# Two gate groups of a hybrid attention layer computed with the activations stationary, and the first loads split over two queues

## The chip, the cores and the metric

The kernel runs on one core of a Trainium2 chip. It is written in a language in which each engine has its own in-order list of instructions: TensorE (PE, matrix products; its weight loads are shown apart as PEld), VectorE (DVE), ScalarE (ACT), GpSimd (POOL) and SyncE (SP). SyncE, GpSimd and ScalarE also issue DMA transfers, each from its own queue. The metric is the device time of one execution in microseconds (us); less is better. Columns streamed by a product are the elements per partition of its moving operand.

## The reference

Two layers work on 256 tokens of width 2048. One input projection of a layer gives eleven parts: queries, keys, values and a gate for eight heads of chunked attention (A); queries, keys, values, a gate and a low-rank forget gate for four heads of gated linear attention (B, "GLA" below); queries and a gate for four heads that attend to 256 memory tokens (M). Each part's output is multiplied by its SiLU gate, and one output projection maps the three back to width 2048.

```python
h = x @ w_in
a_q, a_k, a_v, a_z, b_q, b_k, b_v, b_z, b_lr, m_q, m_z = jnp.split(h, cuts, axis=-1)
y_a = chunk_band_attention(heads_a(a_q), heads_a(a_k), heads_a(a_v), rel_table)   # 8 heads of 128
log_g = log_sigmoid(b_lr @ gate_w + gate_b) / 16
y_b = rms_norm(gla_chunk_recurrence(b_q, b_k, b_v, log_g)) * gla_norm_g           # 4 heads
mk, mv = jnp.split(mem @ w_mem_kv, 2, axis=-1)
y_m = memory_attention(heads_m(m_q), mk, mv)                                      # 4 heads of 128
y = jnp.concatenate([y_a * silu(a_z), y_b * silu(b_z), y_m * silu(m_z)], axis=-1)
x = layer_norm(DEEPNORM_ALPHA * x + y @ w_out, ln_g, ln_b)
```

The sizes are float32 throughout. The part that matters below is `y_a * silu(a_z)`: 1024 columns, which the kernel computes as two groups of 512, `G_AZ0` and `G_AZ1`.

## The kernel before, in words

**Products in three.** Every operand of a large product is split into a high and a low part (`parts`: ScalarE casts the high part, line 117; VectorE subtracts it, line 118), and a product is high times high, low times high and high times low. All such products are issued by the helper `mm`, line 95, so in the profile nearly every product of TensorE bears L95; the tile tells what it belongs to. `acc` is the accumulator of a large group of 512 output columns, `bk` one bank for a head's work or other small work, `wh` and `wl` the two parts of a weight piece, `x` an operand of activations (`xq` the input, `memq` the memory, `yq` the gated output; four tiles each), held transposed, with the contraction on partitions.

**Two forms of a group.** `as_group` keeps the activations stationary: for each of 16 contraction tiles and each half of the 256 tokens, three products of 512 columns (96 in all, in eight pieces of 12); the result has tokens on partitions. `ws_group` keeps the weights stationary: for each contraction tile and each block of 128 output columns one product of 512 columns (the weights' high part on both parts of `x`) and one of 256 (their low part on the high part of `x`), 64 and 64 in eight pieces of 16; its result has output columns on partitions, which is the form in which the heads give their output. Before, `G_AK0`, `G_AK1` and the three gates `G_AZ0`, `G_AZ1` and `G_MZ` are weights-stationary groups. `ws_group` yields two halves; for each, `total` (lines 262 and 263) adds its two sums.

**Turned.** Where a result is needed the other way round, `turned` does it without TensorE: VectorE transposes in blocks of 32 (line 521), GpSimd's queue stores the block to DRAM (`home`, line 523) and reads it back in four loads (line 526) that complete the transposition. Probabilities of a head (`pT`), the GLA output (`yT`) and the queries (`yr`, `qk`) go this way.

**What sets the order.** TensorE's order is that in which the program issues its work. The large groups come one after another: memory keys and values, `G_BQK` (GLA queries and keys), values, queries and keys of A, `G_MQ`, then the gate stage `G_BZ`, `G_AZ0`, `G_AZ1`, `G_MZ`, then the four groups of the output projection `G_WO`. After each piece a group calls `tick`, which advances the generators of the heads: each yields the number of pieces after which it wants its next step. `tick` steps at most one generator per piece, at most two or three are active, and the others stand in `waiting`. A head's step is a visit on TensorE between two pieces: its scores, and about 7 to 9 pieces later the product of its probabilities with the values. `finish(gens)` calls `tick` until the named generators are done. VectorE's and ScalarE's orders are set by a scheduler with priorities; weight pieces (`piece`: loads on SyncE's queue, line 142, and their split) have a high one. There are four buffers of raw pieces and four of each part, so the loads are always some pieces ahead of TensorE. GpSimd's queue is in order too, and its order comes from the scheduler.

**The gate stage before.** `G_BZ` is activation-stationary; its gate multiplies the GLA output with tokens on partitions (`gla_gate`), and `gla_turned` then turns that in two halves and splits it into `yq[0]`. For the three other gates the loop shown in the diff takes both halves' sums through SiLU, calls `finish` for the heads whose output they gate, multiplies (line 901) and splits into `yq[1]` to `yq[3]`. In layer 0 the four loads of the norm's two rows for all partitions (`gb`, lines 917 and 918, on GpSimd's queue) stand in the program in each group of the output projection; their first use is in layer 1, in `restored` (line 632).

**The start.** `zeros` feeds six products whose result nobody reads; they stand ahead of the first real product. `first_pieces` loads, for the first contraction tiles, a block of the memory (`res<-memT`, line 165, into the space that the residual takes later), its value weights (line 178, the very first block in two halves of 256 columns) and its key weights (line 180), in this order and all on SyncE's queue. `gla_inputs` loads the forget gate's weights three times into a 48-row tile (`gwraw`, line 305), its bias (`gb`, line 309) and the GLA norm (`ng`, line 310) on GpSimd's queue. `G_BQK` is followed there by `ident` and `lm`, two constants on SyncE's queue (lines 828 and 830).

Of the kernel before, what the change touches and what calls it, by code (L numbers as in the profile page):

```python
# [36 lines left out]
def hybrid_trunk_kernel(  # L37
# [12 lines left out]
    waiting, active, done, now, linear = [], [], set(), [0], []  # L50
# [103 lines left out]
    def first_pieces(p, x):  # L154
# [9 lines left out]
        def x_part(j):  # L164
            sp.dma_start(xraw[:, j], xsrc[:, j])  # L165
            parts(x[0][:, j], x[1][:, j], xraw[:, j])
# [4 lines left out]
        if p < 2:  # L171
            with tc.manual_schedule(engines={DVE, mybir.EngineType.Activation}):
                for k in range(2):
                    x_part(slice(j0 + k, j0 + k + 1))
                    cut = 2 if p == k == 0 else 1
                    for h in range(cut):
                        cs = slice(h * 512 // cut, (h + 1) * 512 // cut)
                        sp.dma_start(raws[0][:, k, cs], vsrc[:, k, cs])  # L178
                        split(0, (slice(None), k, cs))
# [12 lines left out]
    def first_memory(mk, mv, each):  # L192
# [6 lines left out]
        def values_of(p, w, kk):  # L199

            for h in range(2 if p == kk == 0 else 1):
                cs = slice(h * 256, h * 256 + 256) if p == kk == 0 else slice(0, 512)
                for t in range(2):
                    as_products(accv[:, t, cs], t, memq, [x[:, :, cs] for x in w], p * 2 + kk, kk, -1 if h else 0)
# [93 lines left out]
    def gla_inputs(l):  # L298
# [5 lines left out]
        for i in range(3):  # L304
            pool.dma_start(raw[i * 16:i * 16 + 16], gate_w[l])  # L305
# [3 lines left out]
        pool.dma_start(gb, gate_b[l])  # L309
        pool.dma_start(ng, norm_g[l])  # L310
# [181 lines left out]
    def gla_turned(yraw, ng, y):  # L492

        yT = []
        for par in range(2):
            yT.append(hd.tile([P, 4, P], F32, name=nm("yT"), tag=("gq", "gk")[par]))
            turned(P, (yT[par], yraw[:, 2 * par:2 * par + 2].rearrange("p t d -> p (t d)")))
            yield 6
        for par in range(2):
# [6 lines left out]
            yield 1  # L506

# [270 lines left out]
    for _ in range(6):  # L778
# [6 lines left out]
    for l in range(L):  # L785
# [3 lines left out]
        def staged(g, x, raw, place):  # L789
# [4 lines left out]
            active.append((gen, now[0] + 5))  # L794
# [95 lines left out]
        waiting[:0] = gens[0]  # L890
        for i, g in ((1, G_AZ0), (2, G_AZ1), (3, G_MZ)):
            y = operand()
            gates = []
            for j, a, b in ws_group(w512[l, g], xq):
                sz = scratch([P, 2, T])
                total(sz, a, b)
                act.activation(sz, sz, AF.Silu)
                gates.append((j, sz))
            finish(gens[i])
            for j, sz in gates:  # L900
                dve.tensor_tensor(sz, sz, yraw[i][:, j:j + 2], op=ALU.mult)
                parts(y[0][:, j:j + 2], y[1][:, j:j + 2], sz)
            yq.append(y)
# [5 lines left out]
        gb = []  # L909
        rows = norm_rows(l) if last else None  # L910
        for n in range(WO_N):
            if last:
                g, b = scratch([P, 512]), scratch([P, 512])
            else:
                both = per.tile([P, 2, 512], F32, name=nm("gb"), tag=f"yr{n}")
                g, b = both[:, 0], both[:, 1]
            pool.dma_start(g, ln_g[l:l + 1, columns(n)].to_broadcast([P, 512]))
            pool.dma_start(b, ln_b[l:l + 1, columns(n)].to_broadcast([P, 512]))
            gb.append((g, b))
# [28 lines left out]
            acc = as_group(src, yq, 512)  # L948
# [5 lines left out]
        if not last:  # L954
            norm_between(stats)
# [87 lines left out]
```

## Time and profile before

| what | value |
|---|---|
| time, median of 3 runs | 910.96 us (910.96 to 911.66) |
| the profiled execution's own time | 911.12 us |
| its span in the profile | 909.3 us |
| granted TensorE clock over the span | 0.998 |
| TensorE busy | 902.5 us (99%) |
| weight loads busy (beside products) | 783.0 us (86%) |
| VectorE, ScalarE, GpSimd busy | 606.7, 486.0, 148.1 us |
| DMA traffic | 200.86 MB, mean 221 GB/s |
| packets' share of 16 engines: hardware queue q1, software queue q0 | 60.5%, 10.2% |
| gate stage, layer 0 / layer 1 (end of `G_BZ` to end of `G_MZ`) | 292.0 to 364.0 / 739.8 to 811.7 us |

A busy time is the sum over an engine's instructions of one execution. The chain of waits is followed back from the last instruction, at each step to what released it; a row of it gives start, duration, engine, tile, line and number of instructions. A row of the timeline gives the same for one engine and, in square brackets, how long it had been idle and what it waited for. A row of the windows gives the stretch, its length, the busy time of PE, PEld, DVE, ACT and POOL with their instructions, the granted clock, the DMA engines' busy share and GB/s. A row of the waits says which engine waited for what: total us, number, longest.

### The profile page before, as it was taken

Reading aid. Unit: us, or ns where it says so; the run is one execution under the profiler, and the core shown is the slowest. Engines: PE = TensorE matmul, PEld = TensorE weight load, DVE = VectorE, ACT = ScalarE, POOL = GpSimd, SP = SyncE. Lnnn points to the kernel's source line nnn. Section 1 sums busy time; section 2 is a strip of 40 time slices with the busy share of each in tenths; the row PEclk is TensorE's granted clock in tenths of the full one; section 3 lists DMA queues with packets and bytes.
Section 4 is the critical chain, followed back from the end, with each engine's and each line's share of the span. In section 5 each row is a group of like instructions: output and inputs, shape, how many; then the busy total and the mean of one; then the engine's idle time right before and its main releaser. Section 6 shows DMA issues by size and latency. Waiting matters only on the chain.

```text
span 909.3 us, 14115 instructions
## 1 busy us (share of the span) xinstructions
PE 902.5 (99%) x5116; PEld 783.0 (86%) x5116; DVE 606.7 (67%) x865; ACT 486.0 (53%) x708; POOL 148.1 (16%) x279
## 2 busy tenths in 40 slices
PE   9999999999999999999999999999999999999997
PEld 7889998998888888888888899889888888888885
DVE  5765478757566666655587676885756586876566
ACT  5654475474544666533476445754744365663340
POOL 1002002014142232000000220021141431420000
PEclk9999999999999999999999999999999999999999
DMA  8977875668786778756775687666696966696552
GB/s 292 315 229 213 303 222 185 184 206 272 213 238 215 234 221 257 229 197 195 225 249 177 197 242 209 195 195 208 193 282 192 271 208 212 209 295 212 190 162 93
DMA packets 109365, 200.86 MB, mean 221 GB/s; under 512 B 12136, under 2 KB 72936, under 8 KB 109040
## 3 DMA queue, kind: packets, MB, share of 16 engines
q1 hardware_dynamic: 97920, 173.31, 60.5%
q0 software_dynamic: 11232, 26.40, 10.2%
q8 instruction: 40, 0.66, 0.3%
q10 hardware_dynamic: 144, 0.26, 0.1%
q14 instruction: 29, 0.24, 0.1%
HBM read 186.78 MB, written 13.11 MB: 220 GB/s over the span
## 4 chain that ended last, share of the span: by engine, by line
PE 98%; DMA 1%; SPq 0%; DVE 0%; ACT 0%; issue 0%
PE acc L95 90%; PE bk L95 8%; DMA raw<-w 1%; PE bk L615 0%; SPq L178 0%; PE bk L398 0%; SPq L165 0%; ACT res L771 0%; ACT wh L117 0%; DVE stats L756 0%; PE bk L345 0%; SPq L180 0%; DVE res L755 0%; DVE res L707 0%; DVE mvt L710 0%
## 5 line engine op out<-in xcount | busy, mean ns | idle before, releaser
L95 PE MATMUL acc<-wh,x 128*128 128x512 f32 (+2 forms) x1812 | 538.8, 378 | 0.0
L118 DVE TENSOR_TENSOR wl<-raw,wh 128x1024 fp32r<-128x1024 f32 (+3 forms) x321 | 369.4, 1153 | 207.6 <-ACT wh L117 205.7
L117 ACT CAST wh<-raw 128x1024 fp32r<-128x1024 f32 (+3 forms) x321 | 318.5, 994 | 315.2 <-PE acc L95 244.9
L95 PEld LDWEIGHTS acc<-wh,x 128*128 128x128 f32 x1812 | 334.9, 189 | 48.9 <-issue 0.3
L95 PE MATMUL acc<-wl,x 128*128 128x512 f32 (+2 forms) x906 | 340.8, 376 | 0.0
L95 PE MATMUL acc<-x,wh 128*128 128x512 f32 x672 | 212.2, 397 | 0.1
L95 PEld LDWEIGHTS acc<-wl,x 128*128 128x128 f32 x906 | 170.5, 188 | 26.4 <-DVE wl L118 0.6
L95 PEld LDWEIGHTS acc<-x,wl 128*128 128x128 f32 x672 | 126.2, 188 | 29.7
L95 PE MATMUL acc<-x,wl 128*128 128x256 f32 x672 | 132.2, 278 | 0.0
L95 PEld LDWEIGHTS acc<-x,wh 128*128 128x128 f32 x672 | 103.7, 189 | 1.7 <-ACT wh L117 0.5
L523 POOL DMA_DIRECT2D home<-sc x46 | 25.7, 558 | 397.3 <-DVE sc L521 390.6
L526 POOL DMA_DIRECT2D pT<-home x96 | 52.6, 554 | 51.4 <-DMA home<-sc 29.9
L526 POOL DMA_DIRECT2D yr<-home x48 | 26.1, 551 | 15.1 <-issue 8.0
L545 ACT ACTIVATE sc<-sc,mx 128x128 f32<-128x128 f32 (+1 forms) x32 | 14.4, 450 | 17.2 <-DVE mx L543 17.2
L305 POOL DMA_DIRECT2D gwraw<-gate_w x6 | 3.1, 522 | 105.7 <-PE bk L603 104.9
L387 ACT ACTIVATE sc<-sc 128x512 f32<-128x512 f32 x12 | 7.6, 633 | 14.9 <-DVE sc L385 14.9
L521 DVE STREAM_TRANSPOSE sc<-sc 128x384 f32<-128x384 f32 (+1 forms) x24 | 14.9, 619 | 0.5
L538 DVE SCALAR_TENSOR_TENSOR sc<-bk,bias 128x384 f32<-128x384 f32 x16 | 8.7, 544 | 9.1 <-PE bk L95 9.1
L521 DVE STREAM_TRANSPOSE sc<-acc 128x512 f32<-128x512 f32 x18 | 11.8, 696 | 3.6 <-PE acc L95 3.4
L118 DVE TENSOR_TENSOR x<-sc,x 128x512 fp32r<-128x512 f32 x20 | 13.5, 685 | 0.7 <-ACT x L117 0.7
L526 POOL DMA_DIRECT2D qk<-home x24 | 13.1, 552 | 5.0 <-DMA home<-sc 5.0
L118 DVE TENSOR_TENSOR x<-res,x 128x512 fp32r<-128x512 f32 (+2 forms) x14 | 10.5, 765 | 5.1 <-ACT x L117 5.1
(211 smaller groups left out, 601.0 us busy)
## 6 DMA issues: line engine op xcount, KB each, us to landing
raw<-w SPq DMA_DIRECT2D x142, 512.0 KB, 4.4
raw<-w SPq DMA_DIRECT2D x227, 256.0 KB, 4.0
raw<-w SPq DMA_DIRECT2D x64, 388.0 KB, 3.7
home<-sc POOLq DMA_DIRECT2D x30, 256.0 KB, 4.0
bias<-relw SPq DMA_DIRECT2D x16, 192.0 KB, 4.7
yr<-home POOLq DMA_DIRECT2D x48, 64.0 KB, 4.9
home<-sc POOLq DMA_DIRECT2D x16, 192.0 KB, 3.3
pT<-home POOLq DMA_DIRECT2D x64, 48.0 KB, 4.3
```

The lines of the kernel that those rows point to most:

```text
L95: pe.matmul(o, l, r, start=start, stop=stop, skip_group_check=True)
L117: act.copy(hi, src)
L118: dve.tensor_tensor(lo, src, hi.bitcast(F32), op=ALU.subtract)
L305: pool.dma_start(raw[i * 16:i * 16 + 16], gate_w[l])
L387: act.activation(dd, dd, AF.Abs)
L521: dve.transpose(blocks.rearrange("p b (g j) -> p g b j", j=32), src.rearrange("p (g b j) -> p g b j", b=4, j=32))
L523: pool.dma_start(homes[-1], blocks)
L526: pool.dma_start(dst[b * 32:(b + 1) * 32], home[:, b].rearrange("(a i) n -> i a n", a=4))
L538: dve.scalar_tensor_tensor(s, pb[:, :384], SCALE, bias[h], op0=ALU.mult, op1=ALU.add)
L545: act.activation(s[:, own[t]], s[:, own[t]], AF.Exp, bias=mx[:, t:t + 1], accum_out=zs[:, t:t + 1])
```

## The change

The two gate groups of the chunked attention, `G_AZ0` and `G_AZ1`, become activation-stationary groups in both layers. Their result has tokens on partitions and the heads' output does not, so SiLU's result is turned on its way (`zT`, two stores and eight loads for each group on GpSimd's queue), and the new generator `gated` multiplies it with the heads' output and splits the product. `gated` is stepped from a new list, `side`, in which `tick` steps every generator that is due and which doesn't count against the number of active ones. `gla_turned` and the generators of `staged` (which only place turned queries) move to that list too. The first group of the output projection calls `finish` for the two `gated` at its third and fifth piece. `G_MZ` remains weights-stationary. In layer 0 the norm loads are issued behind the output projection. The five loads of `gla_inputs` move to SyncE's queue. At the start, the first half of the first value weights is loaded by ScalarE's queue, ahead of ScalarE's other work; VectorE instead of ScalarE casts the first memory block; the six products of the first value block are taken by halves of the columns, with both token halves together (the same products in another order); and there are seven idle products.

```diff
+    waiting, active, side, done, now, linear = [], [], [], set(), [0], []
     def tick(share=1.0):
         now[0] += share
+        for e in [e for e in side if e[1] <= now[0]]:
+            side.remove(e)
+            after = next(e[0], None)
+            if after is not None:
+                side.append((e[0], now[0] + after))
+            else:
+                done.add(e[0])
...
         def x_part(j):
             sp.dma_start(xraw[:, j], xsrc[:, j])
-            parts(x[0][:, j], x[1][:, j], xraw[:, j])
+            if p == j.start == 0:
+                dve.tensor_copy(x[0][:, j], xraw[:, j])
+                dve.tensor_tensor(x[1][:, j], xraw[:, j], x[0][:, j].bitcast(F32), op=ALU.subtract)
+            else:
+                parts(x[0][:, j], x[1][:, j], xraw[:, j])
...
+                    if n == 2:
+                        act.dma_start(raws[0][cuts[k][0]], vsrc[cuts[k][0]])
                 for k in range(2):
                     x_part(slice(j0 + k, j0 + k + 1))
+                    for i, at in enumerate(cuts[k]):
+                        if i or len(cuts[k]) == 1:
+                            sp.dma_start(raws[0][at], vsrc[at])
+                        split(0, at)
...
         for i in range(3):
-            pool.dma_start(raw[i * 16:i * 16 + 16], gate_w[l])
+            sp.dma_start(raw[i * 16:i * 16 + 16], gate_w[l])
...
-        pool.dma_start(gb, gate_b[l])
-        pool.dma_start(ng, norm_g[l])
+        sp.dma_start(gb, gate_b[l])
+        sp.dma_start(ng, norm_g[l])
...
             turned(P, (yT[par], yraw[:, 2 * par:2 * par + 2].rearrange("p t d -> p (t d)")))
-            yield 6
+            yield 2 + 4 * par
...
+    def gated(zT, yraw, heads, y):
+        while not all(h in done for h in heads):
+            yield 1
+        for j in range(0, 4, 2):
+            gz = scratch([P, 2, T])
+            for t in range(2):
+                z, o, r = (zT[:, t].rearrange("p a (k j) -> p k a j", j=32)[:, j:j + 2],
+                           *(x[:, :, t * P:(t + 1) * P].rearrange("p k (a j) -> p k a j", j=32) for x in (gz, yraw[:, j:j + 2])))
+                dve.tensor_tensor(o, z, r, op=ALU.mult)
+            parts(y[0][:, j:j + 2], y[1][:, j:j + 2], gz)
...
-    for _ in range(6):
+    for _ in range(7):
         mm(idle[:, :P], zeros, zeros, True, True)
...
-        waiting[:0] = gens[0]
-        for i, g in ((1, G_AZ0), (2, G_AZ1), (3, G_MZ)):
-            y = operand()
-            gates = []
-            for j, a, b in ws_group(w512[l, g], xq):
-                sz = scratch([P, 2, T])
-                total(sz, a, b)
-                act.activation(sz, sz, AF.Silu)
-                gates.append((j, sz))
-            finish(gens[i])
-            for j, sz in gates:
-                dve.tensor_tensor(sz, sz, yraw[i][:, j:j + 2], op=ALU.mult)
-                parts(y[0][:, j:j + 2], y[1][:, j:j + 2], sz)
-            yq.append(y)
+        side.append((gens[0][0], now[0]))
+        need = {}
+        for i, g in ((1, G_AZ0), (2, G_AZ1)):
+            acc = as_group(halves(g), xq, 512)
+            yq.append(operand())
+            zT = hd.tile([P, 2, 4, P], F32, name=nm("zT"), tag="qk", bufs=4)
+            sz = [scratch([P, 512]) for _ in range(2)]
+            for t in range(2):
+                act.activation(sz[t], acc[:, t], AF.Silu)
+            turned(P, *((zT[:, t], sz[t]) for t in range(2)))
+            need[i * 2] = [gated(zT, yraw[i], gens[i], yq[i])]
+            side.extend((x, now[0] + 6) for x in need[i * 2])
...
-            acc = as_group(src, yq, 512)
+            acc = as_group(src, yq, 512, need=need if n == 0 else {})
...
         if not last:
+            for n in range(WO_N):
+                both = per.tile([P, 2, 512], F32, name=nm("gb"), tag=f"yr{n}")
+                gb.append((both[:, 0], both[:, 1]))
+                load_norm(n)
             norm_between(stats)
```

TensorE, layer 0, from the last piece of `G_BZ` (the first two rows) into the first two pieces of `G_AZ0`. In a row stand the line, the operation, the output, the stationary and moving operands as the program names them, the moving operand's partitions and columns, and how often the row is issued in a run; a piece repeats its rows four times. Before:

```order
L95 MATMUL acc_2693<-wh_2919,x_513 128x512 x2
L95 MATMUL acc_2693<-wl_2920,x_513 128x512
...
L95 MATMUL acc_2945<-x_277,wh_2947 128x512 x2
L95 MATMUL acc_2945<-x_277,wl_2948 128x256 x2
...
L95 MATMUL acc_2945<-x_370,wh_2969 128x512 x2
L95 MATMUL acc_2945<-x_370,wl_2970 128x256 x2
```

After:

```order
L102 MATMUL acc_2694<-wh_2920,x_514 128x512 x2
L102 MATMUL acc_2694<-wl_2921,x_514 128x512
...
L102 MATMUL acc_2945<-wh_2947,x_278 128x512 x2
L102 MATMUL acc_2945<-wl_2948,x_278 128x512
...
L102 MATMUL acc_2945<-wh_2975,x_278 128x512 x2
L102 MATMUL acc_2945<-wl_2976,x_278 128x512
```

`G_AZ0`'s products of 256 columns are gone, and each of its pieces is now three products of 512 columns issued four times, as in `G_BZ`. The visits of heads keep their order among the groups, and so does everything else on TensorE.

GpSimd, layer 0, behind the loads of the first two memory heads' probabilities, up to those of the fourth: `yT` is the turned GLA output, `zT` the turned gate, `pT` a memory head's probabilities, `home` the DRAM tile through which each goes, `gb` the norm's rows. Before:

```order
L523 DMA home_3218<-sc_3216 128x512
L526 DMA yT_3215<-home_3218 32x4x128 x4
L917 DMA gb_3824<-ln_g 128x512
L918 DMA gb_3824<-ln_b 128x512
L523 DMA home_3266<-sc_3264 128x512
L526 DMA pT_3263<-home_3266 32x4x128 x4
L523 DMA home_3314<-sc_3312 128x512
L523 DMA home_3416<-sc_3414 128x512
L917 DMA gb_3670<-ln_g 128x512
L918 DMA gb_3670<-ln_b 128x512
L526 DMA pT_3311<-home_3314 32x4x128 x4
L526 DMA yT_3413<-home_3416 32x4x128 x4
```

After:

```order
L559 DMA yT_2965<-home_2968 32x4x128 x4
L559 DMA yT_3012<-home_3015 32x4x128 x4
L556 DMA home_3148<-sc_3146 128x512
L556 DMA home_3152<-sc_3150 128x512
L559 DMA zT_3141<-home_3148 32x4x128 x4
L559 DMA zT_3141<-home_3152 32x4x128 x4
L556 DMA home_3245<-sc_3243 128x512
L556 DMA home_3290<-sc_3288 128x512
L559 DMA pT_3242<-home_3245 32x4x128 x4
L955 DMA gb_4270<-ln_g 128x512
L955 DMA gb_4270<-ln_b 128x512
L559 DMA pT_3287<-home_3290 32x4x128 x4
```

The stores and loads of the GLA output now stand together and ahead, the two stores and eight loads of the first gate stand ahead of the third memory head's store, and one pair of norm loads still stands ahead of the fourth head's `pT`. The second gate's `zT` follows behind these rows.

SyncE, the first loads of the program: `res<-memT` is a block of the memory, `raw` a weight piece's first buffer (here the first two contraction tiles' value and key weights). Before:

```order
L165 DMA res<-memT 128x256
L178 DMA raw_113<-w 128x256 x2
L180 DMA raw_114<-w 128x2x256
...
L178 DMA raw_113<-w 128x512
...
L178 DMA raw_177<-w 128x512
L180 DMA raw_178<-w 128x2x256
```

After:

```order
L172 DMA res<-memT 128x256
L194 DMA raw_114<-w 128x256
L196 DMA raw_115<-w 128x2x256
...
L194 DMA raw_114<-w 128x512
...
L194 DMA raw_178<-w 128x512
L196 DMA raw_179<-w 128x2x256
```

One of the two halves of the first value weights has left this queue; on ScalarE it is the first instruction (L189), ahead of a table load.

More of the change, by code (lines that the diff above doesn't have):

```diff
@@ L793, in staged @@
             gen = placed(raw, place)
-            active.append((gen, now[0] + 5))
+            side.append((gen, now[0] + 5))
             return [gen]
@@ L909, in hybrid_trunk_kernel, with load_norm @@
         gb = []
+        def load_norm(n):
+            for dst, src in zip(gb[n], (ln_g, ln_b)):
+                pool.dma_start(dst, src[l:l + 1, columns(n)].to_broadcast([P, 512]))
         rows = norm_rows(l) if last else None
@@ L912, in hybrid_trunk_kernel @@
             if last:
[L913 to L919, printed above, removed]
+                gb.append((scratch([P, 512]), scratch([P, 512])))
+                load_norm(n)
             src = wo_pieces(l, n)
```

35 lines of the change are left out of this document (25 added, 10 removed).

## The prediction

> **What bounds the kernel now.** I read the page's busy shares and its chain first, then the windows, then the chain row by row around the places the change touches.
>
> ```profile
> span 909.3 us, 14115 instructions
> PE 902.5 (99%) x5116; PEld 783.0 (86%) x5116; DVE 606.7 (67%) x865; ACT 486.0 (53%) x708; POOL 148.1 (16%) x279
> PE 98%; DMA 1%; SPq 0%; DVE 0%; ACT 0%; issue 0%
> 300.00:355.00 55.00, 55.00 (x328) 48.45 (x326) 35.34 (x50) 31.37 (x49) 16.39 (x30) 1.00 0.80 243
> ```
>
> TensorE is busy 99% of the span and carries 98% of the chain. In layer 0's gate stage (300 to 355) it is busy all 55 us, VectorE 64%, ScalarE 57%, the DMA engines 80%. So an edit counts only if it shortens TensorE's own work, makes TensorE wait, or takes away one of its few waits. Two places matter: the price of a product in the two gate groups of each layer, and the first 12 us, where the chain does leave TensorE.
>
> The chain rows of the gates (start, us, what; `acc` are the large groups, `bk` visits of attention heads), the last one from layer 1's output projection:
>
> ```profile
> 285.93 2.76 PE acc L95 x12
> 288.69 0.72 PE bk L95 x6
> ...
> 315.83 2.79 PE acc L95 x16
> 318.62 0.71 PE bk L95 x6
> ...
> 329.13 22.29 PE acc L95 x128
> ...
> 354.93 0.85 PE bk L95 x6
> ...
> 803.45 84.58 PE acc L95 x384
> ```
>
> A weights-stationary group is 64 products of 512 columns and 64 of 256: the 128 in the row of 22.29 us are one group's worth, 0.1741 us each. The row of 384 begins with the last 48 of these (three pieces of G_MZ, 8.36 us); the other 336 are activation-stationary, 512 columns each: (84.58 - 8.36) / 336 = 0.2269 us. A group has 96 of them, 21.78 us. Columns streamed are equal (49,152), but two products of 256 cost more than one of 512.
>
> **The gates, part by part.** Four groups (G_AZ0 and G_AZ1, two layers) change from 22.29 to 21.78: 4 x 0.51 = 2.04 us less TensorE. Visits take some back: after one, a 12-product piece takes 2.75 to 2.76 against 12 x 0.2269 = 2.72, while the 16-product piece after one takes 2.79, which is 16 x 0.1741. Five visits a layer now return into an activation-stationary group: 10 x 0.03 = 0.3. The 354.93 visit took 0.85 where its kind takes 0.72, a wait of 0.13 for late probabilities; it goes if they come in time (below). I take 1.8 from the gates, 0.1 from the visit; bounds 1.4 (visits at 0.06 each, visit still late) and 2.2.
>
> The TensorE page of the Trainium skill, "TensorE: Matmul & The Clock Gate", section "Back-to-back issue gap", gives a warm gap of N / 2.4 + 2.5 ns, so 215.8 at 512 and 109.2 at 256. By that rule four groups would save an estimated 0.3 us only; the rows do not agree with it (226.9 ns at 512, and a 256 that costs over half of that), and rows go first.
>
> What lies beside: the issue price and landings, and the last memory head's way in layer 0.
>
> ```profile
> L523 POOL DMA_DIRECT2D home<-sc x46 | 25.7, 558 | 397.3 <-DVE sc L521 390.6
> home<-sc POOLq DMA_DIRECT2D x30, 256.0 KB, 4.0
> yT<-home POOLq DMA_DIRECT2D x16, 64.0 KB, 4.8
> 337.50 1.12 POOL L523 DMA_DIRECT2D home<-sc  x2
> 338.60 0.54 POOL L917 DMA_DIRECT2D gb<-ln_g  x1
> 343.21 1.66 POOL L526 DMA_DIRECT2D pT<-home  x3 [3.54 <-DMA home<-sc]
> 347.25 0.56 POOL L526 DMA_DIRECT2D pT<-home  x1 [2.38 <-issue]
> 353.78 0.71 ACT L117 CAST sc<-pT 128x256 fp32r<-128x256 f32 x2 [3.18 <-DMA pT<-home]
> L521 DVE STREAM_TRANSPOSE sc<-acc 128x512 f32<-128x512 f32 x18 | 11.8, 696 | 3.6 <-PE acc L95 3.4
> L901 DVE TENSOR_TENSOR sc<-sc,yr 128x512 f32<-128x512 f32 x12 | 8.3, 688 | 3.5 <-ACT sc L897 3.5
> L263 DVE SCALAR_TENSOR_TENSOR sc<-acc,sc 128x512 f32<-128x512 f32 x13 | 8.9, 682 | 0.0
> L118 DVE TENSOR_TENSOR sc<-pT,sc 128x256 fp32r<-128x256 f32 x16 | 6.0, 419 | 3.6 <-ACT sc L117 3.6
> ```
>
> Per group VectorE loses two L263 and two L901 (2.74) and gains two turns of 0.70 and four products of 256 columns, priced by the nearest row at 0.42: 3.1. ScalarE loses two multiplications. Neither is near its limit, so I cost this at nothing; the cover is TensorE's 22 us per group. GpSimd gains, per group, 2 home stores and 8 loads, 10 x 0.55 = 5.5 us of issuing, about 22 in all against its 148 busy.
>
> The turned gates have time. From a group's end: silu and turns 3.5 us, home 4.0 after issue, eight loads 4.4, landing 4.8, so 17 to 18. The product of the two is written six ticks (16.5 us) later, and VectorE, in order, waits a microsecond or so, or up to 4 if it comes early; weight parts stand some 4 us ahead of TensorE there. The projection needs yq[1] only at its third piece, 22 us plus 5 after G_AZ1. The GLA part now has its own place in the side list and is ready a group earlier.
>
> Last memory head: in the old trace its final pT load was issued at 347.25, and ScalarE waited 3.18 us for it until 353.78, just before the visit at 354.93. Nothing is spare there. In the new order the GLA loads are ahead of it by a whole group; zT's two stores and eight loads stand before its store, issued about 8 to 13 us after G_AZ0's end, when that head's scores (11 us after) are only being turned. One gb pair still stands before its loads, as now, waiting for the first gate product. I get loads issued 12 to 14 us and landed 18 to 21 us after the scores; the visit comes 25.5 after.
>
> **Norm loads and gate inputs.** L917's gb pairs in layer 0 move behind zT; first use is in layer 1:
>
> ```profile
> L632 DVE TENSOR_TENSOR res<-res,gb x8: 684/685/689, 514.0 to 551.0; 128x512 f32<-128x512 f32 x8
> SPq L142 <- DVE wl L118: 366.8, 167, 5.3
> 53.83 0.46 SPq L828 DMA_DIRECT2D ident<-ident  x1
> 55.89 0.34 SPq L830 DMA_DIRECT2D lm<-lmask  x1
> 58.66 3.05 SPq L142 DMA_DIRECT2D raw<-w  x3
> ```
>
> They have over 100 us: nothing. Five small loads join SyncE's queue per layer, about 2.3 us of issuing; it waits for buffers 366.8 us over 167 times, and 1.6 and 2.4 us at just this place, so weights behind are at most about 0.4 late against several us of lead: nothing.
>
> **The start.** SyncE issues, GpSimd's first transfers and their queue's row over the first 13 us (packets, MB, share of the 16 engines' time), and the chain:
>
> ```profile
> 0.74 0.39 SPq L165 DMA_DIRECT2D res<-memT  x1
> 1.18 0.89 SPq L178 DMA_DIRECT2D raw<-w  x2
> 1.26 1.61 POOL L305 DMA_DIRECT2D gwraw<-gate_w  x3 [0.82 <-POOLq L1033]
> q0 software_dynamic: 160, 0.05, 1.8%
> 3.35 0.33 PEld L95 LDWEIGHTS bk<-zeros 128*128 128x128 f32 x1
> 3.92 0.50 PEld L95 LDWEIGHTS acc<-wh,x 128*128 128x128 f32 x2 [0.24 <-ACT wh L117]
> 3.58 5.77 DMA raw<-w
> 9.37 0.63 ACT wh L117
> 10.04 0.74 PE acc L95 x2
> 2.50:6.00 3.50, 3.50 (x16) 3.26 (x16) 1.28 (x3) 1.31 (x4) 2.04 (x5) 1.00 0.86 270
> 6.00:9.50 3.50, 3.50 (x18) 3.10 (x18) 1.71 (x3) 1.58 (x4) 0.00 (x0) 1.00 0.94 262
> 9.50:13.00 3.50, 3.38 (x15) 2.14 (x14) 2.45 (x5) 2.70 (x6) 0.00 (x0) 1.00 1.04 385
> ```
>
> Every wait before 13 us ends at a landing: the key piece issued at 3.58 lands at 9.35, is cast, and releases TensorE at 10.04. ScalarE's queue takes the first half piece, so that issue moves up by one, 0.44 us; and GpSimd's five transfers leave: 1.8% of 13 us, 0.23 us on every engine. While these were under way the engines moved 270 and 262 GB/s, afterwards 385. Lower bound: nothing earlier, and the seventh idle product (two passes, about 0.43) starts TensorE 0.2 late: a loss of 0.2. Upper bound: 7 us at 266 GB/s done at 385, 2.2 us. I take 0.7: 0.44 for the issue, which is sure to move, plus 0.23 for the engines' time, the nearest row to GpSimd's part; the rest of the rate difference I leave in the bound. Late next is the value piece behind, on the same engines.
>
> The DMA page, "DMA: Bandwidth & Descriptors", section "Issuing engines are not separate DMA queues", of the Trainium skill says that issuing from several engines saves only issuing time; by it the start would give an estimated 0.44 and the sum 2.3. The queue's row speaks for a little more; no run here yet shows it.
>
> **Sum.** 1.8 + 0.1 + 0.7 = 2.6 us. The profiled execution took 911.12 (span 909.3, 1.8 around it); it becomes 908.5. The median of the three runs, 910.96, lies 0.16 under it: 908.4. What a measurement can tell is 0.2%, 1.82 us: below 909.14 is faster, above 912.78 slower.
>
> **Rivals.**
> First, slower: the last memory head of layer 0 waits behind the added transfers. If zT's stores and loads (5.5 us of issuing) and the wait for their home (4.0) all fall between that head's store and its loads, its probabilities come 9.5 us later than now, where nothing is spare; less the 2.6 gained, 911.0 + 6.9 = 917.9, or 913.9 if only the 5.5 do. It decides when the landing passes 25.5 us after the scores. For it: the 3.18 wait, one in-order queue. Against: zT comes before that head's store, not after. 0.09.
> Second: the gate product reaches VectorE long before zT lands and holds weight parts longer than their 4 us lead. 1.5 to 3 us come back: 909.9 to 911.4. For: in-order VectorE. Against: six ticks, the scores' work before it. 0.09.
> Third: the start gives nothing or loses 0.2, because the landings keep their rate: 909.0 to 909.3, half of it either side of the bound. 0.10.
> Fourth: the extra time of 256-column products belongs to the stage, not the shape, and the new groups take 22.29 as well: 2.04 goes, 910.4. Against: the 2.76 row is in this stage. The page's rule on gaps, cited above, would come out near this. 0.04.
>
> **Numbers.** The forecast, gates 1.4 to 2.2, visit 0.1 and the start 0.3 to 2.2, holds 0.68: 906.5 to 909.2. The range, 906.5 to 910.2, reaches up to take in the third case and the near end of the second and leaves out about 0.19. Faster 0.68 + 0.05 = 0.73, same 0.05 + 0.04 + 0.09 = 0.18, slower 0.09.
>
> **What would show it.** In the new profile: chain rows of 96 `acc` products at 21.8; no `bk` visit over 0.76; PE's 803-type row unchanged; ScalarE's wait for pT in layer 0 gone; the first key release near 9.2 instead of 10.04. Wrong would be any new TensorE wait between 290 and 370, or a first release at 10 again.

## The result and the profile after

The changed kernel took 908.25 us, the median of six runs (908.14 to 908.47), beside 911.64 for the kernel before (six runs, 910.96 to 912.34): a ratio of 0.9964, 95% interval 0.9951 to 0.9977, so 2.1 to 4.5 us less. The two profiled executions differ by 2.8 us in their spans. The page of the changed kernel:

```profile
span 906.5 us, 14032 instructions
PE 899.7 (99%) x4990; PEld 776.9 (86%) x4990; DVE 605.7 (67%) x874; ACT 483.0 (53%) x699; POOL 165.1 (18%) x309
PE 99%; DMA 0%; DVE 0%; ACT 0%; issue 0%
```

TensorE's busy time fell by 2.8, and DMA's share of the chain went from 1% to 0%. Where the time went is read from three places in the two chains (start, us, what). Of the kernel before: the last piece of `G_BZ` with what follows it in layer 0, the same in layer 1, and the work behind the last large groups:

```profile
289.41 19.48 PE acc L95 x108
737.22 19.48 PE acc L95 x108
888.04 11.09 PE bk L95 x60
```

The changed kernel, the same three and more rows of the gates between them:

```profile
288.48 19.08 PE acc L102 x84
324.87 21.99 PE acc L102 x108
350.37 0.71 PE bk L102 x6
735.29 19.08 PE acc L102 x84
797.90 87.37 PE acc L102 x400
885.27 11.09 PE bk L102 x60
```

The changed kernel is 0.93 ahead at the first place (289.41 to 288.48), 1.93 at the second and 2.77 at the third. So 0.93 came from work ahead of the gates, 1.00 between the first place and the second, and 0.84 between the second and the third. The 1.00 and the 0.84 are there by the end of each gate stage (362.08 for 363.99 in layer 0, 808.89 for 811.66 in layer 1), so they belong to the gates. The row of 84 is seven pieces of 12 products at 0.2271 each, so 96 products, a group's worth, are 21.8 us; the last visit in layer 0, 0.85 before, takes 0.71.

The start. Chain rows, a row of TensorE's timeline at the second block of keys, and two windows, whose last numbers are clock, DMA share and GB/s:

```profile
0.73 3.38 DMA raw<-w
4.14 0.41 ACT wh L124
4.60 2.81 PE acc L102 x14
9.72 0.62 PE L102 MATMUL acc<-x,wh 128*128 128x512 f32 x2
6.00:9.50 3.50, 3.50 (x22) 2.88 (x21) 2.67 (x5) 2.21 (x5) 0.00 (x0) 1.00 0.98 271
9.50:13.00 3.50, 3.50 (x19) 2.94 (x18) 2.52 (x5) 2.79 (x5) 0.00 (x0) 1.00 1.04 387
```

From 4.60 the chain stays with TensorE. The key products that waited until 10.04 follow at 9.72 without a wait (no bracket). The DMA rates of these windows are close to those of before, 271 and 387 GB/s for 262 and 385, though GpSimd's five transfers have left them (SyncE issues them from 53.15 on); from 2.5 to 6 us the rate is 285 for 270.

### The profile page after: what moved, and what is told of

Same layout as the page of the kernel before. It is cut to its first block, busy times and chain, and to the rows that moved or that the text cites. A ratio compares the mean times of both kernels' runs of the same rounds, so it can differ in the third digit from the quotient of the medians.

```text
span 906.5 us, 14032 instructions
## 1 busy us (share of the span) xinstructions
PE 899.7 (99%) x4990; PEld 776.9 (86%) x4990; DVE 605.7 (67%) x874; ACT 483.0 (53%) x699; POOL 165.1 (18%) x309
## 4 chain that ended last, share of the span: by engine, by line
PE 99%; DMA 0%; DVE 0%; ACT 0%; issue 0%
PE acc L102 90%; PE bk L102 8%; PE bk L648 0%; DMA raw<-w 0%; PE bk L419 0%; ACT res L804 0%; DVE stats L789 0%; PE bk L366 0%; DVE res L788 0%; ACT wh L124 0%; DVE res L740 0%; DVE mvt L743 0%; PE bk L792 0%; ACT nparts L124 0%; DVE rs_u L751 0%
## 5 line engine op out<-in xcount | busy, mean ns | idle before, releaser
L102 PE MATMUL acc<-wh,x 128*128 128x512 f32 (+2 forms) x2068 | 617.1, 380 | 0.2 <-ACT wh L124 0.2
L102 PEld LDWEIGHTS acc<-wh,x 128*128 128x128 f32 x2068 | 381.8, 188 | 58.7 <-ACT wh L124 0.5
L102 PE MATMUL acc<-wl,x 128*128 128x512 f32 (+2 forms) x1034 | 390.0, 377 | 0.0
L102 PEld LDWEIGHTS acc<-wl,x 128*128 128x128 f32 x1034 | 194.1, 188 | 31.1 <-DVE wl L125 0.3
L102 PE MATMUL acc<-x,wh 128*128 128x512 f32 x416 | 131.2, 397 | 0.0
L102 PEld LDWEIGHTS acc<-x,wl 128*128 128x128 f32 x416 | 78.1, 188 | 18.3
L102 PE MATMUL acc<-x,wl 128*128 128x256 f32 x416 | 81.9, 278 | 0.0
L102 PEld LDWEIGHTS acc<-x,wh 128*128 128x128 f32 x416 | 64.5, 189 | 1.3
L559 POOL DMA_DIRECT2D zT<-home x32 | 17.6, 555 | 20.1 <-DMA home<-sc 10.2
L124 ACT CAST x<-sc 128x512 fp32r<-128x512 f32 x20 | 11.8, 616 | 3.6 <-DVE sc L538 2.3
```

The lines of the kernel that those rows point to most:

```text
L102: pe.matmul(o, l, r, start=start, stop=stop, skip_group_check=True)
L124: act.copy(hi, src)
L559: pool.dma_start(dst[b * 32:(b + 1) * 32], home[:, b].rearrange("(a i) n -> i a n", a=4))
```

## The experiments

The kernels of a group ran on one chip and share runs of the kernel before; the groups are those of four, four, three and one in the order below. Ratios are to the kernel before, with 95% intervals. "G_MZ's stretch" is the time from `G_MZ`'s first product to the output projection's first in layer 0's trace; it is 23.7 us where TensorE doesn't wait.

| kernel | median us | ratio (interval) | G_MZ's stretch |
|---|---|---|---|
| changed | 908.25 | 0.9964 (0.9951 to 0.9977) | 23.7 |
| gates_only | 913.75 | 1.0011 (0.9997 to 1.0025) | 26.5 |
| start_only | 910.52 | 0.9985 (0.9976 to 0.9994) | as before |
| inputs_on_pool | 913.51 | 1.0012 (1.0002 to 1.0022) | 29.1 |
| first_by_sync | 909.42 | 0.9972 (0.9960 to 0.9983) | 23.7 |
| gates_clean | 910.02 | 0.9978 (0.9969 to 0.9987) | 24.5 |
| ng_on_pool | 909.14 | 0.9969 (0.9959 to 0.9978) | 23.8 |
| ng_pool_norms_sync | 909.09 | 0.9966 (0.9954 to 0.9978) | 23.7 |
| inputs_l0_pool | 910.23 | 0.9975 (0.9966 to 0.9984) | 24.3 |
| spare_stores | 910.82 | 0.9990 (0.9976 to 1.0004) | 23.7 |
| keys_too | 913.39 | 1.0016 (1.0003 to 1.0028) | 23.7 |
| gate_product_early | 929.38 | 1.0187 (1.0166 to 1.0208) | 36.3 |
| norms_sync | 909.74 | 0.9970 (0.9959 to 0.9982) | 23.7 |

**The parts alone.** The theory was: gates 1.8, start 0.7, independent. `gates_only`:

```diff
 # the changed kernel with before's first_pieces and values_of, and:
-    for _ in range(7):
+    for _ in range(6):
-            sp.dma_start(raw[i * 16:i * 16 + 16], gate_w[l])
+            pool.dma_start(raw[i * 16:i * 16 + 16], gate_w[l])
 # gb and ng likewise; layer 0's load_norm(n) back in the loop over n
```

> The gate stage as changed (two activation-stationary gates, side list, turned gates), but the start, the forget gate's inputs on GpSimd's queue and the norm loads in the output projection as before. My theory: the gate stages shorten by 0.98 and 0.84 us as in the profile after, and the start keeps its waits, so 1.8 us under the kernel before (ratio 0.9980), the chain's first key products again at about 10.0 us. Rival 'all in the start' (the gates give 0.3 as the page's gap rule has it): 0.2 to 0.4 under before. Rival 'the queue': with the norm loads and gate inputs back on GpSimd's queue the last memory head's probabilities come late, TensorE waits in layer 0 and less than 1 us is gained.

`start_only`:

```diff
 # the kernel before with after's first_pieces and values_of, seven idle products, and:
-            pool.dma_start(raw[i * 16:i * 16 + 16], gate_w[l])
+            sp.dma_start(raw[i * 16:i * 16 + 16], gate_w[l])
 # gb and ng likewise
```

> The start as changed (first half piece by ScalarE's queue, first memory block cast by VectorE, products by halves, seven idle products) and the forget gate's inputs on SyncE's queue; gates and norm loads as before. My theory: 0.7 to 0.9 us under the kernel before (ratio 0.9991), gate groups at 22.3 us as before. Rival 'the start gives nothing alone': within 0.2 of before.

`start_only` gained 0.5 to 2.2 us, in line. `gates_only` gained nothing: the rival of the queue. Its gate groups were as fast as hoped, but TensorE waited in layer 0.

**The start's two halves.** `inputs_on_pool` and `first_by_sync`:

```diff
 # inputs_on_pool: the changed kernel with
-            sp.dma_start(raw[i * 16:i * 16 + 16], gate_w[l])
+            pool.dma_start(raw[i * 16:i * 16 + 16], gate_w[l])
 # gb and ng likewise, both layers
 # first_by_sync: the changed kernel with
-                    if n == 2:
-                        act.dma_start(raws[0][cuts[k][0]], vsrc[cuts[k][0]])
...
-                        if i or len(cuts[k]) == 1:
-                            sp.dma_start(raws[0][at], vsrc[at])
+                        sp.dma_start(raws[0][at], vsrc[at])
```

> The changed kernel with the forget gate's five loads back on GpSimd's queue, all else as changed. My theory, by the engines' time of these transfers: 0.2 us over the changed kernel (0.1 to 0.3), the key piece landing at about 8.2 instead of 7.96. Rival 'rate': these small transfers hold back all others (270 against 385 GB/s), so most of the start's 0.93 comes back, 0.6 to 0.9 over, and TensorE waits for the second key piece at about 9.7 again. Rival 'issue only': no difference.

> The changed kernel with the first half piece back on SyncE's queue, behind the memory block, all else as changed. My theory, by the issue: 0.44 over the changed kernel, all landings behind it 0.4 to 0.5 later. Rival 'rate': the landings are set by the engines' rate from about 2.5 us on, so less than 0.2 over, since TensorE's start hangs on the same bytes.

`first_by_sync`, its chain at the second block of keys:

```profile
3.58 5.82 DMA raw<-w
10.09 0.72 PE acc L102 x2
```

That is the kernel before (3.58, 10.04) without GpSimd's transfers: the place in SyncE's queue sets this release, GpSimd's small loads don't. The theory's size was missed: this key piece was issued 0.48 us later than in the changed kernel (3.58 for 3.10) and landed 1.44 later (9.40 for 7.96), not 0.4 to 0.5. In time its interval overlaps that of the kernels with the full start, so the sizes of the start's parts stay open.

`inputs_on_pool` lost everything, but not at the start: its first product behind the memory groups comes at 49.7 us, in the changed kernel at 49.9. GpSimd's timeline of its layer 0, VectorE's row of the gate product's second half, then its chain, then windows there:

```profile
325.86 0.56 POOL L331 DMA_DIRECT2D ng<-norm_g  x1
328.74 2.23 POOL L559 DMA_DIRECT2D zT<-home  x4 [2.32 <-issue]
337.47 0.54 POOL L955 DMA_DIRECT2D gb<-ln_g  x1 [5.41 <-DVE sc L538]
338.53 3.27 POOL L559 DMA_DIRECT2D pT<-home  x6
...
336.41 0.76 DVE L538 TENSOR_TENSOR sc<-zT,yr 128x256 f32<-128x256 f32 x2 [3.59 <-DMA zT<-home]
...
340.18 9.23 DMA pT<-home
350.19 1.71 PE bk L102 x6
...
349.00:352.00 3.00, 1.81 (x7) 1.81 (x8) 1.64 (x3) 2.57 (x5) 0.00 (x0) 0.67 1.02 354
352.00:356.00 4.00, 4.00 (x22) 3.49 (x22) 2.15 (x4) 1.64 (x5) 1.99 (x4) 0.82 0.73 226
```

Layer 1's `ng`, 512 bytes, stands between the two halves of the turned gate, and 2.3 us pass behind it. The gate product (L538) comes late: its second half waits 3.59 us for `zT`, where in the changed kernel it runs at 332.97 without a wait. A pair of norm loads waits 5.41 us for it, now ahead of both last memory heads' `pT`. Those land 7 to 10 us after their issue, behind the pair's 512 KB (9.23 in the row, the third head's last). TensorE waits 3.6 us for the first of them, and the granted clock is 0.67 and 0.82 in the two windows from 349 to 356. The stretch is 5.3 us longer in all: 3.6 are the wait, the rest is slower work behind it (the visit takes 1.71 us for 0.72, the piece of 16 after it 3.56 for 2.79). It is the place and the effect that the prediction's first rival named, reached by an edit that was costed at nothing.

**Which of these does it?** Four kernels:

```diff
 # gates_clean: gates_only, but in gla_inputs, whose five loads go to q
+        q = (pool, sp)[l]      # layer 0 on GpSimd's queue, layer 1 on SyncE's
 # inputs_l0_pool: the changed kernel with the same line
 # ng_on_pool: the changed kernel with
-        sp.dma_start(ng, norm_g[l])
+        (pool if l else sp).dma_start(ng, norm_g[l])
 # ng_pool_norms_sync: ng_on_pool, and in load_norm
-                pool.dma_start(dst, src[l:l + 1, columns(n)].to_broadcast([P, 512]))
+                (pool if last else sp).dma_start(dst, src[l:l + 1, columns(n)].to_broadcast([P, 512]))
```

> As gates_only (gates as changed; start and norm loads as before), but layer 1's forget-gate inputs go by SyncE's queue, layer 0's still by GpSimd's. What gates_only showed: layer 1's 512-byte norm load (ng) stood on GpSimd's queue between the halves of the turned gate, one pair of norm loads came ahead of both last memory heads' probabilities, and TensorE waited. Theory 'ng': without that load there is no wait, the gate stages shorten by 0.98 and 0.84 and the time is 1.8 us under before (ratio 0.998). Rival 'norm loads in place': the wait stays at 2 to 4 us and the time is no better than before.

> The changed kernel with one edit: layer 1's ng, 512 bytes, is loaded by GpSimd's queue. Theory 'ng': it stands between the halves of the turned gate, the order behind it changes as in inputs_on_pool, TensorE waits 2.5 to 5 us for the last memory heads' probabilities in layer 0: 911 to 913.5, start as in the changed kernel (first chain row at 4.60). Rival 'start': inputs_on_pool was slow by the start's transfers, and this one stays at 908.3 to 909.

> As ng_on_pool, with layer 0's eight norm loads on SyncE's queue behind the output projection's weights: ng still stands between the halves, but nothing on GpSimd's queue waits for the gate product ahead of the probabilities. Theory 'order': the wait was that of the norm pair and of its 512 KB ahead of the probabilities, so it goes: 908 to 909. Rival 'ng alone': the 2.3 us that ng held the queue make the probabilities late, and TensorE still waits 1 us or more: over 909.5.

> The changed kernel with layer 0's forget-gate inputs alone on GpSimd's queue: the five small transfers are back in the first 5 us, and the gate stage is as changed. Theory by the engines' time: 0.1 to 0.3 over the changed kernel. Rival 'rate': 0.6 to 0.9 over, with waits of TensorE before 13 us. Rival 'none': in inputs_on_pool the chain's row after the start was no later than in the changed kernel, so no difference, or 0.2 less.

`gates_clean` shows the gates without the start (layer 1's inputs by SyncE's queue): 1.2 to 2.8 us faster than before. `ng_on_pool` fell against the theory: the same order as `inputs_on_pool`, and hardly a wait, so `ng_pool_norms_sync` had nothing left to cure. `inputs_l0_pool` loses 0.5 us in the gate stage. Its TensorE also waits 0.9 at 9.30, as its rival 'rate' has it, but `gate_product_early` waits 0.8 at 8.57 without these transfers and `inputs_on_pool` doesn't wait there with them. So nothing is shown of what the transfers do at the start.

`ng_on_pool`'s GpSimd rows:

```profile
326.66 0.57 POOL L331 DMA_DIRECT2D ng<-norm_g  x1
327.22 2.17 POOL L559 DMA_DIRECT2D zT<-home  x4
```

No pause follows `ng` here. `gates_clean` has no `ng` there, and a pause all the same (its timeline, then its chain):

```profile
328.92 1.10 POOL L546 DMA_DIRECT2D zT<-home  x2 [2.15 <-issue]
...
342.53 7.34 DMA pT<-home
350.81 1.23 PE bk L102 x6
```

So pause and `ng` are two things. Counting GpSimd's transfers from the program's start, the pause stands ahead of the 118th in every kernel that has layer 0's five small loads on that queue (2.38 us before, 2.25 in `gates_only`, 2.32 in `inputs_on_pool`, 2.15 in `gates_clean` and in `inputs_l0_pool`), whatever the transfer is: a `pT` load in the kernel before, a `zT` load in the others. Two things can be crossed, a pause among the `zT` loads and the norm pair ahead of both heads' `pT`. By the stretch, the pause alone costs 0.5 to 0.8 us (`inputs_l0_pool`, `gates_clean`), the early pair alone 0.1 (`ng_on_pool`), both together 2.8 and 5.3 (`gates_only`, `inputs_on_pool`). The third memory head's last `pT` load shows why. It lands at 341.5 us in the changed kernel, at 344.0 with the pause alone (`gates_clean`), at 345.0 with the pair alone (`ng_on_pool`) and at 349.4 with both (`inputs_on_pool`); the visit that needs it comes at about 347. For this head either delay is covered, the two together are not; the 0.5 to 0.8 of the pause alone are lost at the fourth head's visit behind it.

**A test of the count.** `spare_stores` gives `inputs_on_pool` more to do:

```diff
         values(1)
         if l == 0:
+            spare = drm.tile([P, 9, 16], F32, name="spare", tag="spare", bufs=1)
+            for i in range(9):
+                pool.dma_start(spare[:, i], asv[:, 0, :16])
```

> inputs_on_pool (the forget gate's inputs on GpSimd's queue, TensorE waiting 5.3 us in layer 0's G_MZ) with nine more transfers on GpSimd's queue in layer 0: useless stores of 64 bytes per partition to DRAM, behind the first values group (about 85 us), whose data nobody reads. Theory 'count': GpSimd's queue pauses 2.2 to 2.4 us ahead of its 118th transfer, wherever that falls; nine more ahead move the pause from between the turned gate's halves to the GLA output's last loads, TensorE waits under 1 us, and the kernel with more work is 2 to 5 us faster than inputs_on_pool: 909 to 911 (ratio 0.997 to 0.999). Rival 'ng': the pause belongs to the 512-byte norm load behind which it stood; it stays there, and the time stays at 913 to 914 (ratio 1.001).

GpSimd's rows in layer 0, and the chain at the last visit:

```profile
314.21 1.10 POOL L559 DMA_DIRECT2D yT<-home  x2 [2.08 <-issue]
...
326.36 0.56 POOL L331 DMA_DIRECT2D ng<-norm_g  x1
326.91 2.18 POOL L559 DMA_DIRECT2D zT<-home  x4
...
350.84 0.71 PE bk L102 x6
```

The pause is again ahead of the 118th transfer, which is now a `yT` load; behind `ng` there is none, and the 5.3 us are gone, with `ng` and the early norm pair where they were. The median is 2.7 us lower than that of `inputs_on_pool`, as the theory had it; they ran on two chips, and the intervals of their ratios overlap a little (1.0002 to 1.0004), so the time speaks for it less clearly than the trace.

**More of the same, and the other covers.** `keys_too` has four more groups in the new form, `gate_product_early` takes the second rival's condition, `norms_sync` moves the norm loads:

```diff
 # keys_too: the changed kernel with load_norm as in norms_sync below, and
-            values(2 + half)
             q = hd.tile([P, 4, T], F32, name=nm("qk"), tag="qk", bufs=4)
             laid = staged(G_AQ0 if half == 0 else G_AQ1, xq, yraw[3], lambda src, at, q=q: act.copy(at(q), src))
-            k = heads(G_AK0 if half == 0 else G_AK1)
+            k = hd.tile([P, 4, T], F32, name=nm("qk"), tag="qk", bufs=4)
+            laid = laid + staged(G_AK0 if half == 0 else G_AK1, xq, yraw[2], lambda src, at, k=k: act.copy(at(k), src))
+            values(2 + half)
             finish(laid)
 # gate_product_early: the changed kernel with
-            side.extend((x, now[0] + 6) for x in need[i * 2])
+            side.extend((x, now[0] + 2) for x in need[i * 2])
 # norms_sync: the changed kernel with
-                pool.dma_start(dst, src[l:l + 1, columns(n)].to_broadcast([P, 512]))
+                (pool if last else sp).dma_start(dst, src[l:l + 1, columns(n)].to_broadcast([P, 512]))
```

> The changed kernel with A's four key groups (G_AK0, G_AK1, both layers) activation-stationary and turned as the queries are, each half's values group moved behind its keys so that the turning is covered, and layer 0's norm loads on SyncE's queue. Theory 'price of the form': four more groups save 0.5 us each less 0.03 per visit that returns into one, 1.7 to 2.0 under the changed kernel: 906.3 to 907 (ratio to before 0.994 to 0.995). Rival 'queue': eight more stores and thirty-two more loads on GpSimd's queue make heads' probabilities late, TensorE waits, and it is no faster than the changed kernel. Rival 'page rule' (gap of 2.5 ns per product): 0.3 under.

> The changed kernel with the product of turned gate and heads' output asked for two pieces after a gate group's end instead of six. Second rival of the prediction: VectorE, in order, reaches it 5.4 us after the group's end and waits until the turned gate lands at about 12 to 15 us; weight parts behind it are held up to 9 us, over their lead of about 4 us, so TensorE waits 1.5 to 5 us in each of up to four places: 911 to 920. If the scheduler puts weight parts ahead in VectorE's order all the same: no change, 908.3 to 909.

> The changed kernel with layer 0's eight norm loads on SyncE's queue, behind the output projection's weights; the forget gate's inputs stay on SyncE's queue too, so that no transfer on GpSimd's queue in the gate stage waits for a gate product. My theory: these loads cost nothing where the change left them, since TensorE has no wait in the gate stage, so 908 to 909 and a ratio of 0.996 to 0.997 as for the changed kernel, ScalarE's last wait for probabilities in layer 0 shorter by 1 us or more. Rival 'contention': their 2 MB beside the turned gates lengthen landings that TensorE feels elsewhere, and it is 0.5 us or more faster than the changed kernel; or, behind SyncE's weights, they delay layer 1's first weights and it is slower.

`keys_too` is slower than before by 0.3 to 2.6 us. Two rows of what TensorE waited for (us, times, longest):

```profile
PE bk L102 <- ACT qk L908: 2.4, 3, 1.1
PE acc L102 <- DVE wl L125: 0.9, 3, 0.4
```

The heads wait for the turned keys (L908) and the groups for weight parts. The rival was right that it would be no faster, but what came late was the keys, not the probabilities: a form is worth its price only where the turning is covered. These rows account for 3.3 us; where the rest of the difference to the changed kernel comes from is open.

`gate_product_early`, VectorE's row of layer 0's second gate product, and TensorE's waits:

```profile
360.66 0.76 DVE L538 TENSOR_TENSOR sc<-zT,yr 128x256 f32<-128x256 f32 x2 [5.37 <-DMA zT<-home]
...
PE bk L102 <- DVE sc L125: 7.7, 2, 4.2
PE bk L102 <- ACT sc L124: 7.3, 3, 4.7
```

`G_MZ`'s stretch is 12.6 us longer in layer 0 and 7.8 in layer 1, and the time, 929.38, is well over the expected 911 to 920. The second rival's wait is real: VectorE waits in order for `zT`, and behind it stand the last heads' probabilities, not the weight parts that the rival named (7.7 us of TensorE's waits in the two layers). The 7.3 us in the other row are waits for ScalarE's cast of probabilities, which the rival didn't have: in layer 0 the last head's `pT` loads are issued at 350.22 here and at 339.26 in the changed kernel. Why they come so late is open. The six pieces are what keeps both away.

`norms_sync` is as fast as the changed kernel within the intervals. ScalarE waits no more for `pT` there (0.84 in the changed kernel). But from the output projection's first product of layer 0 to the first product for the norm behind it the trace has 1.2 us more (492 products in 112.7 us for 111.5), some 0.9 of it in gaps between products from 461 to 474 us, one of them a wait for a weight part; this is the slower half of the rival, too small to show in the time. So the norm loads did lie under cover, as expected, although GpSimd issues them from 303.17 to 369.09 in the changed kernel, in the gate stage as before, and not behind the output projection where the program has them. Nothing here beats the changed kernel.

## Why the prediction was right, and where it was not

It gave 908.4 us, faster; 908.25 was measured. That these agree to 0.2 us is in part luck: the forecast took 2.6 from 910.96, while the kernel before, measured again beside the change, had 911.64, so the saving is 3.4 (2.1 to 4.5; 2.8 in the profiles). None of the new TensorE waits between 290 and 370 came that would have shown it wrong.

**The gates (1.8, and 0.1 for the visit): right.** 1.00 and 0.84 in the profiles, `gates_clean` 2.2 us in the median. The new groups cost 21.8 us, and the piece behind a visit takes 2.76 to 2.77 for 2.72, as costed. As the 0.2271 was measured in this stage, the fourth rival, by which the price belongs to the stage, is out. The Trainium skill's rule that the prediction weighed ("TensorE: Matmul & The Clock Gate", "Back-to-back issue gap") would have made it an estimated 0.3; the page gives that formula for an isolated product. The traces don't agree: a product of 512 columns takes 226.9 ns and one of 256 more than half of that.

**The last memory head: right for the changed kernel.** ScalarE's wait of 3.18 us for its probabilities is now

```profile
348.56 0.71 ACT L124 CAST sc<-pT 128x256 fp32r<-128x256 f32 x2 [0.84 <-DMA pT<-home]
```

and the visit follows without a wait. The room was smaller than forecast: its loads were issued 15 to 17 us after the scores' visit and the last landed 24.3 after it, not 12 to 14 and 18 to 21, and the visit comes 26.2 after.

**The start (0.7): the size about right, its two terms not shown apart.** 0.93 in the profiles, 0.5 to 2.2 in `start_only`. The 0.44 for the issue is not told apart from the rest: the second key piece was issued 0.48 earlier than before (3.10 for 3.58), but it landed 1.39 earlier (7.96 for 9.35). By the page of the Trainium skill that was cited ("DMA: Bandwidth & Descriptors", "Issuing engines are not separate DMA queues") only the issuing time is saved; this landing gained more, and no time here is fine enough to decide. The 0.23 for GpSimd's engine time is not shown: with the old order the second key piece lands at 9.35 with these transfers and at 9.40 without (`first_by_sync`), and with the new order the engines moved 291 and 298 GB/s with them (`inputs_on_pool`, 2.5 to 6 and 6 to 9.5 us) and 285 and 271 without. And the rest of the start scatters: the first product behind the memory groups stands at 50.1 to 50.8 us in the profiles with the old start, and at 49.9 to 51.0 in those with the changed start and the inputs on SyncE's queue, so the 0.93 is what this one pair of executions showed. The sign given for the start, a key release near 9.2, was not what came: the last release is that at 4.60, and the keys follow without a wait.

**"Gate inputs: nothing" was the wrong step.** Taken off GpSimd's queue, these loads did three things that were not looked for: they took `ng` from between the turned gate's halves, moved a pair of norm loads behind the third head's `pT`, and, by the count, moved the queue's pause from among the `zT` loads to a place between two stores, where GpSimd's queue waits 5.9 us for VectorE anyhow. With them back, the gates' gain is lost (`gates_only`, `inputs_on_pool`). The question asked was what the move costs SyncE's queue; what it gives GpSimd's was not asked. It didn't show in the number because the change made both moves together; that a move made for the start also kept the gates' gain was luck.

**The first rival** had the right place, one in-order queue ahead of the memory heads' probabilities. What stood there was not what it named: not `zT`'s own transfers between a head's store and its loads, but a norm pair that waited for the gate product, which waited for `zT`; and TensorE waited for the third head first, not for the last. Its price was 5.5 or 9.5 us; the two kernels that came near it show 2.8 and 5.3 in the traces, and medians 1.7 and 1.5 over the kernel before on that chip (913.75 and 913.51 for 912.06), where the rival's near end was 2.9 over.

## What to carry to other kernels

Cost a step for each queue that it leaves as well as for each that it joins: here five small loads, the last of 512 bytes, cost 2.8 and 5.3 us of TensorE's time on an in-order queue that also held a wait for VectorE and a pause, and 0.8 or less where only one of the two delays fell on the probabilities. A group's form can be chosen by the price of a product only where the work it adds is covered by pieces that do not need it; the same exchange that gave 0.5 us a group under the gates gave a loss under the keys. And before a wait is put down to the instruction it stands behind, move that instruction: here the pause belonged to a count of transfers.

## What the runs showed of the hardware

GpSimd's DMA queue paused 2.1 to 2.4 us ahead of its 118th transfer in six kernels with five small loads at the program's start, whichever transfer that was and with nothing in the trace to wait for. In the eight kernels without these loads, the 116th transfer came at least 2.4 us after the one ahead, in three of them with no other reason in the trace (2.5 to 2.6). By the Trainium skill, "DMA: Bandwidth & Descriptors", section "The descriptor swizzle", a transfer of 1 MiB to 128 partitions takes nine read and nine write descriptors on each engine, eight for data and one for completion. An estimate from this, with nine for every transfer here (the loads of `turned` write 32 partitions in four rows each, 128 rows too) and two for one of 16 partitions: 1018 had gone ahead of the one pause and 1021 of the other, so perhaps a ring buffer of 1024 descriptors is full there. No run tested this. Seven of the traces show a further pause of 2.3 us or more that no other engine explains, 106 to 110 transfers later, and this count doesn't explain that one.

After TensorE had waited 3.6 us its granted clock was 0.67 and 0.82 in the windows from 349 to 356, in `inputs_on_pool`; after a wait of 2.3 us in `gates_only` it stayed at 1.00.
